# A hybrid encoder kernel: the exponent rows of the SSD kept twice in memory and loaded by head, and two columns of the input projection moved ahead of four others

## The chip, the cores and the metric

The kernel runs on one core of a Trainium2 chip. The metric is the device time of one execution in microseconds (us). Five engines work beside each other, each in its own order: TensorE (PE) multiplies matrices, VectorE (DVE) and ScalarE (ACT) work element by element, GpSimd (POOL) here mostly issues the DMA loads and stores of activations, SyncE (SP) the loads of weights. They meet at semaphores.

## The reference, cut to what matters

Two sequences of 512 and 256 positions pass through two layers. A layer is one input projection, three branches (a bidirectional state space branch, called SSD here, a windowed attention and a long convolution, called hyena), and one output projection.

```
h = rms_norm(x, norm_g);  u = h @ w_in
z, xbc, dt_raw, q, k, v, g_att, hy_proj, g_hy = split(u)
y_ssd = ssd_branch(z, xbc, dt_raw, ...)      # forward scan + the same on the flipped sequence
y_att = attention_branch(q, k, v, g_att, ...)
y_hy  = hyena_branch(hy_proj, g_hy, ...)     # irfft(rfft(u) * rfft(kern)), times a gate
x = x + concat([y_ssd, y_att, y_hy]) @ w_out

# ssd_scan, on chunks of 128 positions (512 = 4 chunks, 256 = 2 chunks), 16 heads of 64 channels
a_cs   = cumsum(dt * a)                                   # the exponent rows, per head and chunk
y_diag = (cm . bm * exp(a_cs[l] - a_cs[s]), l >= s) @ (x * dt)
y_off  = cm @ prev_state * exp(a_cs)                      # prev_state: scan over chunks
y      = y_diag + y_off
```

## The kernel before, in words

All 768 positions are held at once, 2048 channels as 16 operand tiles. Values are split in a high and a low part (`hi`, `lo` for weights, OPH and OPL for the operand), so that a product is three matmuls. `gemm_col` computes one column of 128 outputs: 16 operand tiles x 2 position halves (PSUM tiles `gs` and `gq`) x 3 products = 96 matmuls of 384 columns. It goes in four quarters of 24 matmuls. ACT makes a `hi` from a raw weight tile (`ACTIVATE hi<-raw`), DVE the `lo` (`lo<-raw,hi`), for 12 matmuls at a time; three buffers of each let the two engines run ahead of PE.

Everything else is background work: generators (`ssd_gen`, `filter_gen`, `hyena_gen`, `att_gen`) from which `gemm` takes one step after each quarter (`bg.step`), and small jobs in the middle of a quarter (`bg.half`, which runs what `bg.mid` holds). Instructions are written in that order. A list scheduler then sets the order on each engine by the order of writing, with weights and their splits raised. Every engine runs its list strictly in order, so an instruction that waits holds all behind it. `bg.flush(g)` runs a generator to its end at once.

The parts that the change touches, with the names that the rows use:

- `ssd_gen` (from L604). The cumulated exponents of 2 directions x 16 heads x 6 chunks are stored to memory as `rows_d` (six stores, L638). Then eight `pair`s of heads run, a new one every fifth step, each in eight steps. A pair loads its rows three times by two (L684, `t<-rows_d`, 256 KB, each row repeated over 128 partitions). It loads them once more for the factor exp(a_cs) of `y_off` (L726), called E2 here: two tiles of 128 partitions x 512, the first 64 partitions for the first head and the others for the second. Each tile takes two loads, of three chunks and of one, and their source is a hand-made address pattern whose outermost size is 2 (heads) and whose second is a 64-fold repeat. `load(out=t, in_=xs_d)` (L746) fetches the branch's input. Three steps later ACT takes the exponential (`t<-t 128x512`, L138) of each tile. In the step after it come the pair's two groups of matmuls into `yS` and `yP` (`m`), and in the last step DVE adds up (`XS<-s,prm_t,m`, the only reader of these two PSUM banks, and `XS<-XS,t`).
- After the columns of the SSD and of the hyena's inputs come the SSD's gates, columns 20 to 27. `scale_ssd` then multiplies the eight tiles XS by a row and stores each (`ys_d<-XS`, L1037).
- Columns 28 to 31 are the hyena's gates. Before a column is used, `bg.flush(hy[j // 2])` runs what is left of a half of the hyena. That half ends with the inverse transform: 48 matmuls `m<-r,t`, whose `r` are split by ACT (`r<-t`) and DVE from four loads of `in_ivS` (L588).
- `new_xs(F32R)` gives the XS buffer anew; its writers wait until all readers of the old one are done, the eight stores to `ys_d` among them. Column 32 (keys) writes `KH` into it by four ACT copies (`XS<-s 64x768`), column 33 (values) fills `vt`. Then attention and the columns 34 to 37 follow.
- All `load`s of activations stand in one queue on POOL, in order.

Of the kernel before, what the change touches and what calls it, by code (L numbers as in the profile page):

```python
# [11 lines left out]
F32 = mybir.dt.float32  # L12
F32R = mybir.dt.float32r
# [6 lines left out]
DEPTH = 2  # L20
TH = 384
D = 2048
SL, PL = 512, 256
# [74 lines left out]
def trunk(ctx: ExitStack, tc: tile.TileContext, xT, w_in, w_dt, w_out, prm, brow, w1, mlpv, w2, w3, w4,  # L98
# [22 lines left out]
    def t2(shape=(128, 512), dt=F32):  # L121
        return t2p.tile(list(shape), dt, tag="t2", name="t2")
# [4 lines left out]
    def TT(o, a, b, op, eng=None):  # L127
        (eng or nc.vector).tensor_tensor(out=o, in0=a, in1=b, op=op)  # L128
# [5 lines left out]
    def STT(o, a, s, b, op0, op1, eng=None):  # L134
        (eng or nc.vector).scalar_tensor_tensor(out=o, in0=a, scalar=s, in1=b, op0=op0, op1=op1)  # L135
# [33 lines left out]
    def new_xs(dt=F32):  # L169
        xs_tile[:] = [big.tile([128, 8 * T], dt, tag="XS", name="XS")]  # L170

    def XS(j, a=0, b=T):
        return xs_tile[0][:, T * j + a:T * j + b]
# [6 lines left out]
    fb_d = drp.tile([8, 128, 512], F32, name="fb_d")  # L180
    f0_d = drp.tile([8, 512], F32, name="f0_d")
    rows_d = drp.tile([DEPTH, 2, 16, NCH, 128], F32, name="rows_d")
    ys_d = drp.tile([DEPTH, 8, 128, T], F32, name="ys_d")
    xs_d = drp.tile([DEPTH, 8, 128, T + GAP], F32, name="xs_d")

# [2 lines left out]
    def P(l, base, i):  # L188
        c = l * NPRM + base + i
        return prm_t[:, c:c + 1]  # L190
# [85 lines left out]
    def gemm_col(src, consume):  # L276
        out = banks()
        gemm([src], [out])
        consume(*out)
# [324 lines left out]
    def ssd_gen(l, dtT, BT, CT, ready):  # L604
# [22 lines left out]
        TT(adt, dt, bc(na, (128, 2, NCH, 16)), MUL)  # L627
        yield
        yield
        for b in range(3):  # L630
            p = mp((16, 4, 128))
            for i in range(4):
                c, d = divmod(4 * b + i, 2)
                MM(p[:, i, :], adt[:, d, c, :], tri_t[:, d, :])
            r = t2((16, 4, 128))
            nc.scalar.copy(out=r, in_=p)
            for d in range(2):
                load(out=rows_d[l, d, :, 2 * b:2 * b + 2, :],  # L638
                     in_=r.rearrange("h (c d) t -> h d c t", d=2)[:, d])
        p = mp((128, 2, 2, NCH, 16))  # L640
        for d in range(2):
            MM(p[:, 0, d], tri_t[:, d, :], adt[:, d])
# [10 lines left out]
        TS(acs[:, 1], acs[:, 1], -1.0, MUL)  # L653
        yield
        yield

        FW, BW = (0, 1, 2, 4), (1, 2, 3, 5)

        def group(g):
            bt, cbF, cbB = s3((128, NCH, 128)), s3((128, NCH, 128)), s3((128, NCH, 128))  # L660
# [13 lines left out]
        def pair(j, bt, cbF, cbB):  # L674
# [44 lines left out]
            prep(0, R0)  # L719
            R2 = rows(2)  # L720
            E2 = []
            for d, cs in ((0, BW), (1, FW)):
                t = t2((128, 4, 128))
                for i, n in ((0, 3), (3, 1)):
                    src = rows_d[l, d, h0:h0 + 2, cs[i]:cs[i] + n, :]
                    load(out=t[:, i:i + n, :], in_=bass.AP(src.tensor, src.offset,  # L726
                         [[NCH * 128, 2], [0, 64], [128, n], [1, 128]]))
                E2.append(t)
            yield
            H = [t2((128, 4, 2, 64)), t2((128, 4, 2, 64))]  # L730
# [23 lines left out]
            for c in range(NCH):  # L754
                for hh in range(2):
                    hs = slice(64 * hh, 64 * hh + 64)
                    o = yS[hs, c, :] if c < 4 else yP[hs, c - 4, :]
                    MM(o, X[:, c, hh, :], Ms[c // 2][:, hh, c % 2, :])
            yield
            dsk = P(l, PDS, j)  # L760
            yT = Xf.rearrange("p (c t) -> p c t", c=NCH)
            STT(yT[:, 0:4], t[:, 0:SL].rearrange("p (c t) -> p c t", c=4), dsk, yS, MUL, ADD)
            STT(yT[:, 4:6], t[:, SL + GAP:T + GAP].rearrange("p (c t) -> p c t", c=2), dsk, yP, MUL, ADD)
            for d, cs in ((0, BW), (1, FW)):
                for i, n in ((0, 3), (3, 1)):
                    c = cs[i]
                    TT(yT[:, c:c + n], yT[:, c:c + n], E2[d][:, i:i + n], ADD)
            yield

        act, nxt, gt = [], 0, None  # L770
# [196 lines left out]
    for l in range(DEPTH):  # L967
# [57 lines left out]
        for j in range(8):  # L1025
            def f(ps, pq):
                z = silu2(ps, pq, rstd)
                y = XS(j)
                TT(y, y, z, MUL)
                square_acc(y, acc, j == 0)  # L1030
# [5 lines left out]
                TT(y, y, r, MUL)  # L1036
                load(out=ys_d[l, j], in_=y)  # L1037
        rms(acc, 1024, eps4, 2, scale_ssd)
        for j in range(4):
            def f(ps, pq):  # L1040
                bg.flush(hy[j // 2])
                a = hconv(j, ps, pq)
                TT(yh[j][:, 0:SL], yh[j][:, 0:SL], a[:, 0:SL], MUL)
                TT(yh[j][:, SL:T], yh[j][:, SL:T], a[:, SL + GAP:T + GAP], MUL)
            gemm_col(W(28 + j), f)

        new_xs(F32R)
        KH = [XS(6), XS(7)]
        kL = s3p.tile([128, T], F32R, tag="s3", name="kL")
        KL = [(kL[:, 0:SL], kL[:, SL:T]), (t2((128, SL), F32R), t2((128, PL), F32R))]  # L1050

        def f(ps, pq):
            k = s3()
            evac(lambda a, b: k[:, a:b], ps, pq, rstd)
            for g in range(2):
                ks = k[64 * g:64 * g + 64]
                for o in (g, 1 - g):
                    ACT(KH[g][64 * o:64 * o + 64], ks, AF.Copy)
                hi = KH[g][64 * g:64 * g + 64].bitcast(F32)
                for o in (g, 1 - g):  # L1060
                    for t, a, b in zip(KL[g], (0, SL), (SL, T)):
                        TT(t[64 * o:64 * o + 64], ks[:, a:b], hi[:, a:b], SUB)
# [3 lines left out]
        def f(ps, pq):  # L1066
# [8 lines left out]
                    nc.scalar.copy(out=vt[:, 3 * b:3 * b + 3, :], in_=p)  # L1075
            bg.later(4, turn)
        gemm_col(W(33), f)
        qs, QA = [], [[XS(2 * i % 6), XS(2 * i % 6 + 1)] for i in range(4)]
        bg.add(att_gen(l, qs, QA, KH, KL, vt))
        for i in range(4):  # L1080
# [193 lines left out]
```

## Time and profile before

| | us |
|---|---|
| median of 3 runs | 2487.45 (2485.87 to 2487.83) |
| the profiled execution | 2489.0 |
| its span in the trace | 2487.2 |
| PE busy in the span | 2441.4 |
| DVE busy | 1580.5 |
| ACT busy | 1087.5 |
| POOL busy | 341.4 |

PE is busy nearly all the time, so the time is PE's work, at the clock that was granted, plus PE's gaps. The busy time of another engine counts only where PE waits for it. The list of waits of PE therefore is the list of what could be saved, and the granted clock (PEclk, 1.00 is 2.4 GHz, 0.50 is 1.2 GHz) is the second thing to look at.

### The profile page before, as it was taken

The page shows a single profiled execution, that of the slowest core. Times are in us where ns is not written, and L with a number is a line of the kernel's source. Part 1 is how long each engine was busy: PE and PEld are TensorE (multiplying, and loading weights), DVE is VectorE, ACT ScalarE, POOL GpSimd, SP SyncE. Part 2 cuts the span into 40 slices and gives each one's busy share as a digit, 9 for nine tenths or more (in the row PEclk, how much of TensorE's full clock was granted, in tenths as well). Part 3 has the DMA queues.
Part 4 walks back from the last instruction along what each step waited for, and adds up shares of the span by engine and source line. Part 5 has one row for each costly group of instructions (what it writes and reads, how often), then busy time and mean ns, then how long its engine had stood idle before and what let it go on. Part 6 is the DMA issues. An engine that isn't in the chain of part 4 may idle for free.

```text
span 2487.2 us, 40924 instructions
## 1 busy us (share of the span) xinstructions
PE 2441.4 (98%) x15066; PEld 2393.2 (96%) x15066; DVE 1580.5 (64%) x3410; ACT 1087.5 (44%) x2560; POOL 341.4 (14%) x683
## 2 busy tenths in 40 slices
PE   8999999999999999999999999999999999999998
PEld 7999999999999999999999999999999999999997
DVE  6888775558856766544476787766746477573333
ACT  6467653334334444333353575633332355352332
POOL 2033221221100010121200332201001000000001
PEclk9999999999999999999999999999999999999999
DMA  4266542443421132344421555423213111332223
GB/s 169 63 153 146 142 129 86 129 133 124 140 78 60 51 100 80 112 149 132 146 96 55 141 149 149 135 85 106 94 60 128 63 54 47 106 109 89 77 82 132
DMA packets 126921, 266.22 MB, mean 107 GB/s; under 512 B 30175, under 2 KB 36666, under 8 KB 126720
## 3 DMA queue, kind: packets, MB, share of 16 engines
q1 hardware_dynamic: 78048, 136.35, 17.7%
q0 software_dynamic: 48672, 127.26, 17.2%
q8 instruction: 118, 1.93, 0.3%
q14 instruction: 83, 0.68, 0.1%
HBM read 231.23 MB, written 34.18 MB: 107 GB/s over the span
## 4 chain that ended last, share of the span: by engine, by line
PE 90%; DMA 4%; issue 2%; DVE 1%; ACT 1%; POOL 1%; DVEq 0%; ACTq 0%; POOLq 0%
PE gs L141 38%; PE gq L141 38%; PE m L141 12%; DMA t<-rows_d 3%; PE m L848 1%; PE gl L141 1%; POOL t L726 0%; ACT t L138 0%; DMA XS<-in_xT 0%; DMA s<-in_xT 0%; ACT hi L138 0%; DVE lo L128 0%; DVE t L135 0%; PE m L1000 0%; DVE t L128 0%
## 5 line engine op out<-in xcount | busy, mean ns | idle before, releaser
L138 ACT ACTIVATE hi<-raw 128x256 fp32r<-128x256 f32 x984 | 405.6, 414 | 1040.1 <-PE gq L141 920.5
L128 DVE TENSOR_TENSOR lo<-raw,hi 128x256 fp32r<-128x256 f32 x984 | 412.5, 421 | 597.9 <-ACT hi L138 587.0
L141 PE MATMUL gs<-OPH,hi 128*128 128x384 f32 x1920 | 657.4, 342 | 18.1 <-ACT OPH L138 11.0
L141 PE MATMUL gs<-OPH,lo 128*128 128x384 f32 x1920 | 645.0, 336 | 0.6 <-DVE lo L128 0.5
L141 PE MATMUL gq<-OPH,lo 128*128 128x384 f32 x1920 | 644.4, 336 | 0.0
L141 PE MATMUL gs<-OPL,hi 128*128 128x384 f32 x1920 | 644.0, 336 | 0.1
L141 PE MATMUL gq<-OPH,hi 128*128 128x384 f32 x1920 | 644.1, 335 | 0.0
L141 PE MATMUL gq<-OPL,hi 128*128 128x384 f32 x1920 | 643.3, 335 | 0.0
L141 PEld LDWEIGHTS gs<-OPH,hi 128*128 128x128 f32 x1920 | 362.4, 189 | 25.2 <-ACT OPH L138 11.3
L141 PEld LDWEIGHTS gs<-OPH,lo 128*128 128x128 f32 x1920 | 361.6, 188 | 2.7 <-DVE lo L128 2.7
L141 PEld LDWEIGHTS gs<-OPL,hi 128*128 128x128 f32 x1920 | 362.3, 189 | 0.8 <-DVE OPL L135 0.6
L141 PEld LDWEIGHTS gq<-OPH,hi 128*128 128x128 f32 x1920 | 361.8, 188 | 0.0
L141 PEld LDWEIGHTS gq<-OPL,hi 128*128 128x128 f32 x1920 | 361.6, 188 | 0.0
L141 PEld LDWEIGHTS gq<-OPH,lo 128*128 128x128 f32 x1920 | 361.5, 188 | 0.0
L128 DVE TENSOR_TENSOR t<-t,t 128x512 f32<-128x512 f32 (+3 forms) x260 | 169.1, 668 | 26.5 <-ACT t L138 23.6
L135 DVE SCALAR_TENSOR_TENSOR s<-cv,prm_t,s 128x770 f32<-128x770 f32 x144 | 145.9, 1015 | 22.6 <-ACT s L138 21.9
L138 ACT ACTIVATE t<-s,dt 128x128 f32<-128x128 f32 x384 | 133.6, 391 | 18.9 <-DVE t L135 18.5
L128 DVE TENSOR_TENSOR s<-s,s 128x768 f32<-128x768 f32 (+2 forms) x126 | 112.8, 904 | 27.3 <-ACT s L138 26.7
L138 ACT ACTIVATE t<-t 128x512 fp32r<-128x512 f32 (+3 forms) x132 | 77.3, 587 | 92.4 <-DMA t<-rows_d 48.6
L128 DVE TENSOR_TENSOR t<-m,t 128x256 f32<-128x256 f32 (+3 forms) x157 | 72.3, 485 | 18.3 <-PE m L141 5.8
L684 POOL DMA_DIRECT2D t<-rows_d x96 | 68.8, 719 | 103.9 <-DVE XS L128 38.0
L138 ACT ACTIVATE t<-t,acs 128x128 f32<-128x128 f32 x192 | 73.6, 389 | 13.6 <-DVE t L135 13.6
(225 smaller groups left out, 2572.6 us busy)
## 6 DMA issues: line engine op xcount, KB each, us to landing
raw<-in_w_in SPq DMA_DIRECT2D x368, 256.0 KB, 3.0
raw<-in_w_out SPq DMA_DIRECT2D x128, 256.0 KB, 3.0
t<-rows_d POOLq DMA_DIRECT2D x96, 256.0 KB, 6.4
s<-in_xT POOLq DMA_DIRECT2D x24, 384.0 KB, 4.4
xs_d<-s POOLq DMA_DIRECT2D x16, 385.0 KB, 4.2
s<-xs_d POOLq DMA_DIRECT2D x16, 385.0 KB, 9.3
t<-rows_d POOLq DMA_DIRECT2D x32, 192.0 KB, 10.5
t<-in_decay POOLq DMA_DIRECT2D x24, 256.0 KB, 4.9
```

Of the source, the lines that this page charges most:

```text
L128: (eng or nc.vector).tensor_tensor(out=o, in0=a, in1=b, op=op)
L135: (eng or nc.vector).scalar_tensor_tensor(out=o, in0=a, scalar=s, in1=b, op0=op0, op1=op1)
L138: nc.scalar.activation(o, i, f, **kw)
L141: nc.tensor.matmul(o, lhsT=l, rhs=r, start=start, stop=stop)
L684: load(out=t, in_=rows_d[l, d, h0:h0 + 2, 2 * u:2 * u + 2, :].partition_broadcast(128))
L848: nc.tensor.transpose(pt[g][:, 128 * kb:128 * kb + 128], s[g][:, 128 * kb:128 * kb + 128], ident)
```

## The change

Three things are changed.

First, a second tensor `ed_d` holds the exponent rows in the order in which E2 reads them: per direction and head four chunks of 128. Six more stores a layer fill it, beside those to `rows_d`. E2's loads become one for each tile and head, 128 KB of the row of one head, repeated over 64 partitions. There are four loads a pair, as before.

Second, the last step of a pair becomes a function `final` that is put into `bg.mid`. The pair's generator ends one step sooner.

Third, the columns 32 and 33 are computed ahead of 28 to 31, and the new XS buffer is taken inside the use of column 32.

```diff
--- before.py
+++ after.py
@@ -180,6 +180,7 @@
     fb_d = drp.tile([8, 128, 512], F32, name="fb_d")
     f0_d = drp.tile([8, 512], F32, name="f0_d")
     rows_d = drp.tile([DEPTH, 2, 16, NCH, 128], F32, name="rows_d")
+    ed_d = drp.tile([DEPTH, 2, 16, 4, 128], F32, name="ed_d")
     ys_d = drp.tile([DEPTH, 8, 128, T], F32, name="ys_d")
     xs_d = drp.tile([DEPTH, 8, 128, T + GAP], F32, name="xs_d")
 
@@ -627,6 +628,7 @@
         TT(adt, dt, bc(na, (128, 2, NCH, 16)), MUL)
         yield
         yield
+        FW, BW = (0, 1, 2, 4), (1, 2, 3, 5)
         for b in range(3):
             p = mp((16, 4, 128))
             for i in range(4):
@@ -635,8 +637,11 @@
             r = t2((16, 4, 128))
             nc.scalar.copy(out=r, in_=p)
             for d in range(2):
-                load(out=rows_d[l, d, :, 2 * b:2 * b + 2, :],
-                     in_=r.rearrange("h (c d) t -> h d c t", d=2)[:, d])
+                v = r.rearrange("h (c d) t -> h d c t", d=2)[:, d]
+                load(out=rows_d[l, d, :, 2 * b:2 * b + 2, :], in_=v)
+                cs = [(i, c - 2 * b) for i, c in enumerate((BW, FW)[d]) if c // 2 == b]
+                i, c = cs[0]
+                load(out=ed_d[l, d, :, i:i + len(cs), :], in_=v[:, c:c + len(cs)])
         p = mp((128, 2, 2, NCH, 16))
         for d in range(2):
             MM(p[:, 0, d], tri_t[:, d, :], adt[:, d])
@@ -654,8 +659,6 @@
         yield
         yield
 
-        FW, BW = (0, 1, 2, 4), (1, 2, 3, 5)
-
         def group(g):
             bt, cbF, cbB = s3((128, NCH, 128)), s3((128, NCH, 128)), s3((128, NCH, 128))
             for b in range(2):
@@ -719,12 +722,10 @@
             prep(0, R0)
             R2 = rows(2)
             E2 = []
-            for d, cs in ((0, BW), (1, FW)):
+            for d in range(2):
                 t = t2((128, 4, 128))
-                for i, n in ((0, 3), (3, 1)):
-                    src = rows_d[l, d, h0:h0 + 2, cs[i]:cs[i] + n, :]
-                    load(out=t[:, i:i + n, :], in_=bass.AP(src.tensor, src.offset,
-                         [[NCH * 128, 2], [0, 64], [128, n], [1, 128]]))
+                for hh in range(2):
+                    load(out=t[64 * hh:64 * hh + 64], in_=ed_d[l, d, h0 + hh].partition_broadcast(64))
                 E2.append(t)
             yield
             H = [t2((128, 4, 2, 64)), t2((128, 4, 2, 64))]
@@ -756,15 +757,16 @@
                     hs = slice(64 * hh, 64 * hh + 64)
                     o = yS[hs, c, :] if c < 4 else yP[hs, c - 4, :]
                     MM(o, X[:, c, hh, :], Ms[c // 2][:, hh, c % 2, :])
-            yield
-            dsk = P(l, PDS, j)
-            yT = Xf.rearrange("p (c t) -> p c t", c=NCH)
-            STT(yT[:, 0:4], t[:, 0:SL].rearrange("p (c t) -> p c t", c=4), dsk, yS, MUL, ADD)
-            STT(yT[:, 4:6], t[:, SL + GAP:T + GAP].rearrange("p (c t) -> p c t", c=2), dsk, yP, MUL, ADD)
-            for d, cs in ((0, BW), (1, FW)):
-                for i, n in ((0, 3), (3, 1)):
-                    c = cs[i]
-                    TT(yT[:, c:c + n], yT[:, c:c + n], E2[d][:, i:i + n], ADD)
+            def final():
+                dsk = P(l, PDS, j)
+                yT = Xf.rearrange("p (c t) -> p c t", c=NCH)
+                STT(yT[:, 0:4], t[:, 0:SL].rearrange("p (c t) -> p c t", c=4), dsk, yS, MUL, ADD)
+                STT(yT[:, 4:6], t[:, SL + GAP:T + GAP].rearrange("p (c t) -> p c t", c=2), dsk, yP, MUL, ADD)
+                for d, cs in ((0, BW), (1, FW)):
+                    for i, n in ((0, 3), (3, 1)):
+                        c = cs[i]
+                        TT(yT[:, c:c + n], yT[:, c:c + n], E2[d][:, i:i + n], ADD)
+            bg.mid.append(final)
             yield
 
         act, nxt, gt = [], 0, None
@@ -1036,20 +1038,13 @@
                 TT(y, y, r, MUL)
                 load(out=ys_d[l, j], in_=y)
         rms(acc, 1024, eps4, 2, scale_ssd)
-        for j in range(4):
-            def f(ps, pq):
-                bg.flush(hy[j // 2])
-                a = hconv(j, ps, pq)
-                TT(yh[j][:, 0:SL], yh[j][:, 0:SL], a[:, 0:SL], MUL)
-                TT(yh[j][:, SL:T], yh[j][:, SL:T], a[:, SL + GAP:T + GAP], MUL)
-            gemm_col(W(28 + j), f)
-
-        new_xs(F32R)
-        KH = [XS(6), XS(7)]
-        kL = s3p.tile([128, T], F32R, tag="s3", name="kL")
-        KL = [(kL[:, 0:SL], kL[:, SL:T]), (t2((128, SL), F32R), t2((128, PL), F32R))]
+        KH, KL = [], []
 
         def f(ps, pq):
+            new_xs(F32R)
+            KH.extend((XS(6), XS(7)))
+            kL = s3p.tile([128, T], F32R, tag="s3", name="kL")
+            KL.extend(((kL[:, 0:SL], kL[:, SL:T]), (t2((128, SL), F32R), t2((128, PL), F32R))))
             k = s3()
             evac(lambda a, b: k[:, a:b], ps, pq, rstd)
             for g in range(2):
@@ -1075,6 +1070,14 @@
                     nc.scalar.copy(out=vt[:, 3 * b:3 * b + 3, :], in_=p)
             bg.later(4, turn)
         gemm_col(W(33), f)
+        for j in range(4):
+            def f(ps, pq):
+                bg.flush(hy[j // 2])
+                a = hconv(j, ps, pq)
+                TT(yh[j][:, 0:SL], yh[j][:, 0:SL], a[:, 0:SL], MUL)
+                TT(yh[j][:, SL:T], yh[j][:, SL:T], a[:, SL + GAP:T + GAP], MUL)
+            gemm_col(W(28 + j), f)
+
         qs, QA = [], [[XS(2 * i % 6), XS(2 * i % 6 + 1)] for i in range(4)]
         bg.add(att_gen(l, qs, QA, KH, KL, vt))
         for i in range(4):
```

How instructions move, at three places.

The first place is POOL's queue in layer 0, where the second pair's loads are issued. `h_d<-s` is the store of an intermediate of the filter's network; `s<-xs_d`, `t<-rows_d` and `t<-ed_d` are the pair's loads. Before:

```order
L375 DMA h_d<-s_1643 128x768
L746 DMA s_1714<-xs_d 128x770
L684 DMA t_1832<-rows_d 128x2x256
L684 DMA t_1834<-rows_d 128x2x256
L684 DMA t_1915<-rows_d 128x2x256
L684 DMA t_1917<-rows_d 128x2x256
L726 DMA t_1919<-rows_d 128x1x384
L726 DMA t_1919<-rows_d 128x1x128
L726 DMA t_1922<-rows_d 128x1x384
L726 DMA t_1922<-rows_d 128x1x128
```

After:

```order
L687 DMA t_1839<-rows_d 128x2x256
L747 DMA s_1721<-xs_d 128x770
L687 DMA t_1841<-rows_d 128x2x256
L687 DMA t_1922<-rows_d 128x2x256
L687 DMA t_1924<-rows_d 128x2x256
L728 DMA t_1926<-ed_d 64x512 x2
L728 DMA t_1929<-ed_d 64x512 x2
L118 MEMSET cv 128x2 x3
L376 DMA h_d<-s_1650 128x768
```

The store `h_d<-s` stood ahead of all these loads and now stands behind them.

The second place is ACT's list in layer 0, at the end of the hyena's second half, where the inverse's splits `r<-t` stand; `t_7424<-t_7412` and the like are the other operand of the same matmuls. Before:

```order
L526 COPY t_7399<-m 128x256
L527 COPY t_7399<-m 128x256
L138 ACTIVATE hi<-raw 128x256 x3
L138 ACTIVATE t_7424<-t_7412 128x512
L138 ACTIVATE t_7428<-t_7413 128x512
L138 ACTIVATE r_7436<-t_7434 128x512
L138 ACTIVATE r_7442<-t_7440 128x512
L138 ACTIVATE r_7472<-t_7470 128x512
L138 ACTIVATE r_7478<-t_7476 128x512
```

After:

```order
L527 COPY t_7413<-m 128x256
L528 COPY t_7413<-m 128x256
L138 ACTIVATE hi<-raw 128x256 x5
L138 ACTIVATE t_7487<-t_7475 128x512
L138 ACTIVATE t_7491<-t_7476 128x512
L138 ACTIVATE hi<-raw 128x256 x2
L138 ACTIVATE r_7499<-t_7497 128x512
L138 ACTIVATE r_7505<-t_7503 128x512
L138 ACTIVATE r_7603<-t_7601 128x512
L138 ACTIVATE r_7609<-t_7607 128x512
```

Between the last copies of the forward transform and the inverse's splits stood three weight splits, and now stand seven. On PE the 48 matmuls of this inverse came 35 weight matmuls behind the last of the forward transform, and now come 81 behind; the first half's inverse stood 80 behind in the kernel before.

The third place is ACT's list in layer 1, behind the last row of the SSD's norm (`s<-m,eps`). Before, the first gate of the hyena followed:

```order
L138 ACTIVATE s_19771<-m,eps_93 128x512
L138 ACTIVATE s_19771<-m,eps_93 128x256
L138 ACTIVATE hi<-raw 128x256 x8
L138 ACTIVATE s_19940<-cv,prm_t 128x770
L138 ACTIVATE hi<-raw 128x256 x4
```

After, the four key copies into the new XS buffer:

```order
L138 ACTIVATE s_19784<-m,eps_93 128x512
L138 ACTIVATE s_19784<-m,eps_93 128x256
L138 ACTIVATE hi<-raw 128x256 x9
L138 ACTIVATE XS<-s_19950 64x768
L138 ACTIVATE hi<-raw 128x256
L138 ACTIVATE XS<-s_19950 64x768 x2
L138 ACTIVATE hi<-raw 128x256
L138 ACTIVATE XS<-s_19950 64x768
L138 ACTIVATE hi<-raw 128x256 x9
```

The copies stand one column behind the norm, between weight splits; in the kernel before they came four columns later. On PE the order of the weight matmuls and of the SSD's matmuls around them is as before. On DVE the pair's last step (`XS<-s,prm_t,m`) stands behind the same weight matmul in both kernels.

## Rows read from the trace of the kernel before

**Rows 1.** Page, busy time: us (share of the span) and instructions.

```profile
PE 2441.4 (98%) x15066; PEld 2393.2 (96%) x15066; DVE 1580.5 (64%) x3410; ACT 1087.5 (44%) x2560; POOL 341.4 (14%) x683
```

**Rows 2.** Waits of PE, whole span: us in total, times, longest us.

```profile
PE m L141 <- DVE XS L135: 7.9, 2, 4.0
PE gs L141 <- ACT hi L138: 6.5, 5, 2.1
PE m L141 <- ACT r L138: 4.6, 1, 4.6
```

**Rows 3.** Timeline of PE: start, us, instruction [idle before, releaser].

```profile
276.36 0.80 PE L141 MATMUL m<-t,s 128*128 128x128 f32 x2 [4.00 <-DVE XS L135]
...
355.21 0.45 PE L141 MATMUL gs<-OPH,hi 128*128 128x384 f32 x1 [1.44 <-ACT hi L138]
...
1604.95 0.45 PE L141 MATMUL gs<-OPH,hi 128*128 128x384 f32 x1 [2.03 <-ACT hi L138]
```

**Rows 4.** Waits of ACT, the row on the exponent rows: us, times, longest.

```profile
ACT t L138 <- DMA t<-rows_d: 48.6, 24, 4.7
```

**Rows 5.** Timeline of ACT, at E2's exponentials.

```profile
274.25 0.63 ACT L138 ACTIVATE t<-t 128x512 f32<-128x512 f32 x1 [2.00 <-DMA t<-rows_d]
274.79 1.01 ACT L138 ACTIVATE hi<-raw 128x256 fp32r<-128x256 f32 x3
...
1603.96 0.63 ACT L138 ACTIVATE t<-t 128x512 f32<-128x512 f32 x1 [3.08 <-DMA t<-rows_d]
```

**Rows 6.** Timeline of DVE behind them.

```profile
275.22 0.42 DVE L128 TENSOR_TENSOR lo<-raw,hi 128x256 fp32r<-128x256 f32 x1 [7.89 <-ACT hi L138]
```

**Rows 7.** Timeline of POOL: issues of E2's loads, and the store ahead of them.

```profile
165.35 0.56 POOL L375 DMA_DIRECT2D h_d<-s  x1 [11.02 <-ACT hi L138]
...
262.43 3.23 POOL L726 DMA_DIRECT2D t<-rows_d  x4 [0.35 <-issue]
...
1592.90 3.22 POOL L726 DMA_DIRECT2D t<-rows_d  x4 [3.36 <-PE m L141]
```

**Rows 8.** Page, DMA issues: count, KB each, median us from issue to landing.

```profile
t<-rows_d POOLq DMA_DIRECT2D x96, 256.0 KB, 6.4
t<-rows_d POOLq DMA_DIRECT2D x32, 192.0 KB, 10.5
...
ys_d<-XS POOLq DMA_DIRECT2D x16, 384.0 KB, 4.8
...
rows_d<-t POOLq DMA_DIRECT2D x12, 16.0 KB, 2.7
```

**Rows 9.** Windows: length, busy of PE, PEld, DVE, ACT, POOL; PEclk, DMA share, GB/s.

```profile
1600.20:1602.20 2.00, 2.00 (x22) 1.75 (x22) 0.00 (x0) 0.64 (x1) 0.00 (x0) 1.00 0.19 61
1587.00:1590.00 3.00, 3.00 (x20) 3.00 (x19) 3.00 (x10) 1.29 (x4) 1.42 (x2) 1.00 0.71 203
```

**Rows 10.** Windows behind five of PE's gaps, columns as above.

```profile
189.90:193.40 3.50, 3.47 (x11) 3.21 (x12) 3.47 (x9) 3.50 (x11) 0.00 (x0) 0.52 0.22 75
276.30:282.10 5.80, 5.74 (x23) 5.74 (x24) 4.64 (x14) 2.55 (x7) 0.72 (x1) 0.51 0.33 88
...
695.60:702.00 6.40, 6.38 (x28) 6.08 (x29) 5.32 (x12) 3.11 (x5) 1.23 (x5) 0.51 0.09 12
1526.60:1531.60 5.00, 4.99 (x25) 4.99 (x26) 3.84 (x11) 1.75 (x5) 0.72 (x1) 0.66 0.33 95
1604.90:1612.00 7.10, 7.05 (x34) 6.89 (x35) 5.09 (x15) 5.55 (x19) 0.00 (x0) 0.76 0.36 120
```

**Rows 11.** Timeline of PE, inverse transforms of the hyena's second and first half.

```profile
695.61 8.94 PE L141 MATMUL m<-r,t 128*128 128x256 f32 x48 [4.58 <-ACT r L138]
...
619.57 2.65 PE L141 MATMUL m<-r,t 128*128 128x256 f32 x21
```

**Rows 12.** Timeline of POOL in layer 1, the last store of the SSD's output.

```profile
1878.79 0.54 POOL L1037 DMA_DIRECT2D ys_d<-XS  x1 [0.67 <-DVE XS L128]
```

**Rows 13.** Timeline of ACT in layer 1, a weight split just behind.

```profile
1885.12 0.42 ACT L138 ACTIVATE hi<-raw 128x256 fp32r<-128x256 f32 x1 [1.67 <-PE gq L141]
```

## The prediction

> **What bounds the kernel now.** I read the page's busy times first. PE is busy 2441.4 us of a span of 2487.2 [rows 1], so 45.8 us are PE's gaps, and the rest of the engines matter only where they make one. Next the waits of PE. Three of their rows stand in the part of the program that is changed [rows 2]: 7.9 us in two waits for DVE's last step of a pair, 6.5 us in five waits for a weight split `hi`, 4.6 us in one wait for the hyena's `r`. The other 26.8 us of gaps are not on the change's path, and I leave them alone.
>
> The timelines say what these gaps are. The reader should follow one from the end. At 276.36 PE had waited 4.00 us for a PSUM bank that DVE's last step frees [rows 3]. DVE had stood idle for 7.89 us, not with that step but with the weight split `lo` ahead of it, which waited for ACT's `hi` [rows 6]. ACT made that `hi` at 274.79, right behind the exponential of the second E2 tile, and this had waited for its load [rows 5]. The load had been issued from 262.43 on [rows 7]. So PE's gap is the landing of E2, 11.8 us after the first of four issues, and DVE and ACT only hand it on. The other gaps have the same chain: 1604.95 with an exponential at 1603.96 and loads issued from 1592.90 (11.1 us), 355.21 [rows 3], and the second wait for DVE's step, before 1526.6 [rows 2, 10]. In all ACT waits 48.6 us in 24 waits for such rows [rows 4]; most of these waits are absorbed by splits made ahead, the rest is PE's.
>
> Behind the gaps comes a second cost. The granted clock is 0.51 in the 5.8 us after the gap of 276.36, and 0.52, 0.51, 0.66 and 0.76 in the stretches after four others [rows 10]: PE ran at 1.2 GHz in a part of each of these stretches, where 2.4 GHz is full speed.
>
> **The change, part by part.**
>
> *E2 by head.* Needed first: how early must the tiles land? At 276.36 a last exponential 4.00 us earlier starts at 270.25, 7.8 us after the first issue. At 1604.95 it is 2.03 us earlier, 1601.9, or 9.0 us after it [rows 3, 5, 7]. How long will the new loads take? No row has a 64-partition load of repeated rows. The nearest above is the 256 KB load of `rows_d` over 128 partitions, 6.4 us against 10.5 for the old 192 KB load [rows 8]: the smaller old load is the slower one. The nearest below is the 16 KB store, 2.7 us [rows 8]. A new load moves 128 KB. Halfway between the two is 4.6 us, and the last of four is issued three times 0.81 us behind the first (3.23 us for four [rows 7]), so it lands after some 7.0 us; with the whole 6.4 us it is 8.8. The first is in time at both places, the second is 1 us late at the earlier one and in time at the other. What speaks for the lower value: the old load runs narrow. While only its tail was under way the DMA share was 0.19 at 61 GB/s, where `rows_d` loads of the ordinary form run at 0.71 and 203 GB/s [rows 9].
>
> The Trainium skill has a rule for that: its page "DMA: Bandwidth & Descriptors", section "Rules for kernel authors", says that an outermost size below 16 confines a transfer to at most that many engines. The old pattern has 2 outermost, the new one 64; the share of 0.19 agrees with a narrow transfer.
>
> So the gain is both waits for DVE's step, 7.9, and of the 6.5 us of `hi` waits 5.5: 2.03 and 1.44 [rows 3], and the longest, 2.1 [rows 2], before 189.9. That last one also has another remedy: the store `h_d` held POOL 11.02 us until 165.35 [rows 7] with all of the second pair's loads behind it, and now stands behind them. I leave 1 us out of the 6.5, two small waits that I don't follow. Sum 13.4; for the residue above I take off 0.6 (bounds 0 and 2).
>
> *The clock* comes back with the gaps. One minus the clock, times the length, is 1.7, 2.8, 3.1, 1.7 and 1.7 over the five windows [rows 10], 11.0 in all. The window says a bit too much: 48 matmuls of the inverse took 8.94 us, where 21 at full speed took 2.65, or 6.06 for 48 [rows 11]. That is 2.9 lost where the window says 3.1. With this factor 10.2, of which 3.1 x 0.92 = 2.9 belong to the hyena's gap and 7.3 to E2's.
>
> *Stores.* Six stores a layer of under 16 KB, each about 0.54 us of issue on POOL as another store takes [rows 12], 3 us a layer. They stand between the six to `rows_d`, ahead of the first pair's loads. What hides them is PE's own columns, which ask nothing of POOL. Cost 0; if the first pair's loads come 3 us later and nothing takes it up, 3 us a layer, which I count in the upper end.
>
> *The last step in `bg.mid`.* DVE's order of this step is the same, so it neither moves the step nor frees the banks sooner. What it does: the generator ends 24 matmuls sooner, and the filter's work in layer 0 starts sooner and mixes differently. Value 0.5 lost, bounds 2 either way, the size of the small gaps that work has now.
>
> *Keys and values first.* The gain is at the hyena's second half in layer 0. Its inverse stood 35 weight matmuls behind the forward, with four splits `r` in a row behind the last loads, and PE waited 4.6 us [rows 2, 11]. Now the distance is 81, as at the first half, whose inverse at 619.57 runs on without a gap [rows 11]. So 4.6 go, and with them 2.9 of clock. Layer 1 has no such gap and gains nothing.
>
> The price is a new wait. The four key copies on ACT write the new XS buffer and so wait for all eight stores to `ys_d`. The last is issued at 1878.79 [rows 12] and lands 4.8 us later by the median [rows 8], at 1883.6. The first copy stands 18 weight matmuls behind that issue. A matmul of 256 columns takes 0.126 us (21 in 2.65 [rows 11]), one of 384 then some 0.19, so 18 are 3.4 us, and ACT waits about 1.4. Queued behind it is `hi`, and behind that PE. ACT waited 1.67 us for PE to free a buffer before a `hi` in this stretch [rows 13], so it is as far ahead as the buffers let it. Two full ones hold 24 matmuls, 4.6 us of work. A wait of 1.4 is covered. If the last store landed 4 us later than the median, 1 us would be missing; I put the bound at 4 us a layer, and take 0.5 for both.
>
> **Sum.** 13.4 - 0.6 (E2) + 4.6 (hyena) + 10.2 (clock) - 0.5 (filter) - 0.5 (keys) = 26.6. The profiled execution took 2489.0, so 2462.4; it lies 1.55 above the median of the runs. Forecast 2460.9, say 2461. Own range 2457 to 2465.
>
> **Rivals.**
>
> B, the loads only get halfway: they land 1 to 2 us late at the tight places, gaps of 1 to 2 us stay at three of them and with them some clock. 5 to 11 us are lost of the 26.6, 2466 to 2472. For it: each pair's tiles stand behind other loads in one queue, and their issue isn't earlier. Against: the 9.0 us at one of the two places.
>
> C, the keys' wait: it exceeds the cover, 2 to 4 us a layer plus a low clock of 1.7 to 3 behind each [rows 10], 5 to 14 in all, 2466 to 2475. For it: the eight stores are issued 1 us apart and queue among themselves. Against: ACT's idle time before each split [rows 13].
>
> D, the new loads are no faster, since a load into 64 partitions gains nothing on one into 128. Then E2's gaps and their clock stay, and only the hyena's 4.6 + 2.9 and little else is won: 2480 to 2481.
>
> The Trainium skill speaks for D: "SBUF — State Buffer", section "Door 1", has 64 partitions reach only half of the ports, and the rules of the DMA page advise against splitting a transfer into partition halves. By that the 6.4 us of a full load would hold for each half or be doubled. No row here shows a 64-partition load large enough to say.
>
> E, slower: the same mechanism, but the new loads land later than the old. It decides from about 13 us after the first issue, against 11.8 now: of the 24 waits of ACT [rows 4] twelve end a pair, and if each grows by 1.1 us and PE pays it, the 7.5 us of the hyena and 5 us more are lost. At 15 us the time would be 2489 - 8 + 12 x 3.2, about 2518. For it only the halves; against it the narrow old pattern [rows 9].
>
> F, the change doesn't do what it says: for the second part this is my forecast (the order is the same); for the first it is D.
>
> **How the numbers follow.** Forecast 0.68, B 0.12, C 0.10, D 0.06, E 0.04. The likeliest is the forecast, 2461. The range reaches down to 2456 (the filter's 2 us and a residue of 0) and up over most of B and C, to 2474. A measurement of this kernel can tell about 0.2%, 5 us, from no change. Faster is below 2482.5: the forecast, B, C and most of D, 0.91. Within 0.2%: the slower side of D, the milder of E, 0.05. Slower 0.04.
>
> **What would show it.** Right: the waits of PE of the changed kernel have no row of 3 us or more for DVE's last step and none for `r`; ACT's wait for `ed_d` is below 15 us in all, against 48.6; the new loads' median to landing is below 6.4 us; PEclk is 1.00 between 150 and 2400 us. Wrong: ACT's wait for `ed_d` near 40 (D); a row of ACT waiting for the `ys_d` stores with PE waiting for `hi` behind it (C); new gaps in the filter's stretch around 500 to 560 us.

## The result and the profile after

The changed kernel took 2458.23 us (median of four, 2457.56 to 2459.86) against 2487.34 for the kernel before on the same chip: ratio 0.9885 (0.9868 to 0.9902), 29.1 us less. The forecast was 2461, its own range 2457 to 2465. The time is right, in part by luck: in the profiled execution the keys cost 5.0 us more than forecast, and misses of 2.7, 1.7 and some 3.6 us the other way made up for it.

The waits of PE over the whole span, after (us in total, times, longest):

```profile
PE gs L141 <- ACT OPH L138: 10.8, 2, 9.7
PE m L141 <- ACT t L138: 2.0, 3, 1.0
PE m L141 <- DVE t L128: 1.9, 1, 1.9
PE m L141 <- DVE s L128: 1.1, 1, 1.1
PE gs L141 <- DVE lo L128: 0.6, 1, 0.6
...
```

The three rows of [rows 2] are gone. The largest left is the start, which the change doesn't touch. The 1.9 us for `t` are new.

ACT's wait for the exponent rows, which was 48.6 us [rows 4], and the page's rows on the loads (count, KB each, median us to landing), after:

```profile
ACT t L138 <- DMA t<-ed_d: 3.3, 5, 1.5
```

```profile
t<-rows_d POOLq DMA_DIRECT2D x96, 256.0 KB, 6.1
...
t<-ed_d POOLq DMA_DIRECT2D x64, 128.0 KB, 6.4
```

The place that the prediction followed, on POOL and on ACT, after:

```profile
256.69 2.08 POOL L728 DMA_DIRECT2D t<-ed_d  x4
```

```profile
261.98 0.62 ACT L138 ACTIVATE t<-t 128x512 f32<-128x512 f32 x1
262.91 0.63 ACT L138 ACTIVATE t<-t 128x512 f32<-128x512 f32 x1 [0.31 <-DMA t<-ed_d]
```

The second exponential starts 6.2 us after the first issue, where it started 11.8 us after [rows 5, 7]. By the prediction it may start up to 7.8 us after it without a gap on PE, and there is none here. The four loads took 3.8 to 4.6 us each from issue to landing. Half of the pairs' loads, issued right behind loads of `rows_d`, took 7.5 to 10.8 us, so the median is 6.4. Four windows over the SSD's stretches (length, busy of PE, PEld, DVE, ACT, POOL; PEclk, DMA share, GB/s) show PE busy nearly throughout and the clock at 1.00, i.e. 2.4 GHz:

```profile
150.00:240.00 90.00, 89.29 (x599) 86.79 (x599) 81.78 (x196) 65.29 (x185) 27.26 (x60) 1.00 0.60 163
240.00:380.00 140.00, 139.76 (x940) 136.97 (x939) 110.45 (x266) 82.32 (x233) 33.84 (x74) 1.00 0.48 137
1360.00:1560.00 200.00, 200.00 (x1344) 197.09 (x1343) 170.91 (x411) 136.89 (x390) 55.51 (x116) 1.00 0.58 156
1560.00:1640.00 80.00, 80.00 (x524) 79.16 (x523) 54.98 (x122) 34.60 (x91) 9.82 (x28) 1.00 0.33 104
```

**Where the time went.** Each of the 11648 weight matmuls `gs` and `gq` stands in all traces. The start of the same-numbered one says what a stretch gave against the profiled execution of the kernel before, its clock included. The last column is a second execution of the changed kernel, the run `e8_after` of the next section.

| stretch | weight matmuls | us, after minus before | second execution |
|---|---|---|---|
| start | 0 to 624 | -1.8 | -1.3 |
| SSD pairs, layer 0 | 624 to 1488 | -12.5 | -11.1 |
| filter and hyena's first half, layer 0 | 1488 to 2832 | -2.2 | -2.4 |
| key copies, layer 0 | 2832 to 2904 | +5.5 | +2.0 |
| hyena's second half, layer 0 | 2904 to 3144 | -7.0 | -7.1 |
| rest of layer 0, start of layer 1 | 3144 to 6528 | -1.3 | -1.4 |
| SSD pairs, layer 1 | 6528 to 7416 | -9.3 | -9.6 |
| rest | 7416 to the end | -0.5 | -0.5 |

The start is not the change's: a gap of 1.2 us that stands there in every execution ended between 16.4 and 18.5 us, in kernels that are alike there.

The +5.5 is the price of the keys in this execution. ACT, DVE and PE there, after, in three views:

```profile
633.73 2.57 ACT L138 ACTIVATE XS<-s 64x768 fp32r<-64x768 f32 x3 [3.64 <-DMA t<-in_fwS]
636.33 0.42 ACT L138 ACTIVATE hi<-raw 128x256 fp32r<-128x256 f32 x1
...
638.27 0.61 ACT L138 ACTIVATE t<-t 128x512 fp32r<-128x512 f32 x1
```

```profile
634.61 2.05 DVE L128 TENSOR_TENSOR kL<-s,XS 64x512 fp32r<-64x512 f32 x4 [3.08 <-ACT XS L138]
...
641.16 0.69 DVE L128 TENSOR_TENSOR t<-t,t 128x512 fp32r<-128x512 f32 x1
```

```profile
638.94 0.73 PE L141 MATMUL m<-r,t 128*128 128x256 f32 x4 [0.80 <-ACT t L138]
641.90 0.79 PE L141 MATMUL m<-r,t 128*128 128x256 f32 x2 [1.88 <-DVE t L128]
```

ACT waited 3.64 us before the first key copy. The view names a load of `in_fwS`, but the two such loads under way landed at 634.15 and 634.78, after the copy had begun; the last store to `ys_d` was issued at 627.28 and landed at 633.43, 0.3 us before it. Behind the copies stood the split `t<-t`, which the forward transform of the hyena's second half waits for (two expectations below call it an inverse; the first half's inverse was done by 607 us). DVE's second half of that split came behind the eight subtractions for the keys. PE was without work twice, 2.7 us in all, and the window behind the second gap has the clock at 0.57:

```profile
641.90:648.70 6.80, 6.80 (x28) 6.80 (x29) 2.44 (x6) 1.47 (x4) 0.00 (x0) 0.57 0.13 42
```

In layer 1 ACT waits at the same place, but only weight splits stand behind the copies there, and PE has no gap:

```profile
1855.01 0.85 ACT L138 ACTIVATE XS<-s 64x768 fp32r<-64x768 f32 x1 [2.79 <-DMA t<-fb_d]
```

### The profile page after: what moved, and what is told of

Read it like the earlier page. It is cut to its first block, busy times and chain, and to the rows that moved or that the text cites. A ratio compares the mean times of both kernels' runs of the same rounds, so it can differ in the third digit from the quotient of the medians.

```text
span 2458.1 us, 40960 instructions
## 1 busy us (share of the span) xinstructions
PE 2430.2 (99%) x15066; PEld 2384.6 (97%) x15066; DVE 1583.1 (64%) x3410; ACT 1088.3 (44%) x2560; POOL 327.9 (13%) x695
## 4 chain that ended last, share of the span: by engine, by line
PE 92%; issue 3%; DMA 2%; DVE 1%; POOL 1%; ACT 1%; DVEq 0%; POOLq 0%; ACTq 0%
PE gs L141 39%; PE gq L141 38%; PE m L141 13%; PE m L850 1%; PE gl L141 1%; DMA t<-rows_d 1%; DMA t<-in_fwS 0%; PE m L1002 0%; DMA t<-in_w 0%; DMA prm_t<-in_prm 0%; ACT t L138 0%; DVE dt L135 0%; DMA XS<-ys_d 0%; PE m L502 0%; DVE s L135 0%
## 5 line engine op out<-in xcount | busy, mean ns | idle before, releaser
L141 PE MATMUL gs<-OPH,hi 128*128 128x384 f32 x1920 | 655.7, 342 | 11.0 <-ACT OPH L138 10.8
L141 PEld LDWEIGHTS gs<-OPH,hi 128*128 128x128 f32 x1920 | 361.5, 188 | 16.9 <-ACT OPH L138 11.1
```

What stands on the lines that cost most here:

```text
L141: nc.tensor.matmul(o, lhsT=l, rhs=r, start=start, stop=stop)
```

## The experiments

The theory: the old E2 loads were slow because of their address pattern; the keys pay a wait for the stores; the rest follows. The rivals: the order in memory or the place in the queue made the old loads slow; the keys' own work makes the gap; the last step in the middle of a quarter has a part in the gain.

**Each part alone.** The first: `ed_d`, its stores and the loads by head, all else as before.

> The kernel before with the second tensor ed_d and the loads by head alone (last step and columns as before). If the E2 loads were the cause of the gaps before matmuls of the SSD, all of them go with their low clock and nothing else changes: between the same weight matmuls of layer 0 and layer 1 some 22 us less than before, 2463 to 2467 us; the gap of 4.6 us before the hyena's inverse stays. If the gain of the whole change came in part from the last step in the middle of a quarter, less: 2470 or more.

Measured 2464.74 us against 2489.46, ratio 0.9904 (0.989 to 0.9919), 24.7 less. ACT waited 3.3 us for `ed_d`. The rows of PE's waits for DVE's last step and for `hi` were gone, and the row for the hyena's `r` stood as before. In the profiled execution the two stretches of the pairs took 14.0 and 9.0 us less. So this part carries most of the gain, and by itself.

```profile
ACT t L138 <- DMA t<-ed_d: 3.3, 4, 1.8
```

```profile
PE m L141 <- ACT r L138: 4.6, 1, 4.6
```

The third: the columns 32 and 33 ahead of 28 to 31.

> The kernel before with the key and value columns ahead of the hyena's gates alone. Theory: the gap of 4.6 us before the inverse of the second half goes with 3 us of clock (7.5 us), and a new one comes at the key copies, which wait for the stores to ys_d, 5.4 us with its clock: net 2 us, 2484 to 2486. If the key copies cost nothing by themselves and the gap in the changed kernel had another cause: 2479 to 2481.

Measured 2486.01, ratio 0.9989 (0.998 to 0.9999), 3.4 less. The wait for `r` was gone, and the gap of 1.9 us for `t` at the keys was there, without a low clock behind it. In the profiled execution the hyena's stretch took 5.5 us less and the keys' 1.1 more, so here the keys paid back a part of the gain, not most of it. Another 2.0 went in the stretch behind.

```profile
PE m L141 <- DVE t L128: 1.9, 1, 1.9
```

The second: the last step in `bg.mid`.

> The kernel before with the pair's last step in the middle of a quarter alone. DVE's order of that step is the same, so the gaps at the pairs stay as they are (7.9 us for DVE's last step, 6 to 7 us for hi). What can move is the filter's work of layer 0, which starts one quarter sooner: if the 1.8 us of small waits between 480 and 580 us that the changed kernel does not have went with it, 2 us less than before; if they went with another part, no difference and the waits are still there.

Measured 2483.17, ratio 0.9973 (0.9964 to 0.9982), 6.2 less, where I had forecast next to nothing and then expected 2. Of the waits between 480 and 580 us only one row of 1.4 us was left. The more interesting row is the hyena's second inverse, which this part doesn't name at all. PE, timeline:

```profile
689.94 0.51 PE L141 MATMUL m<-r,t 128*128 128x256 f32 x2 [2.83 <-ACT r L138]
```

The gap was 4.58 [rows 11], and 3.4 us at 1.2 GHz followed it, where 6.8 had. The order of the instructions says why: the generator of a pair ends a quarter sooner, all background work behind it moves up, and the second half's forward transform ends 48 weight matmuls ahead of its inverse, not 35. By the weight matmuls this part took 2.0 us out of the filter's stretch and 3.0 out of 2832 to 3144; the start's scatter of 1.8 was lost again in other stretches, so its profiled execution gained 4.9 in all. The pairs' own gaps stayed, 4.4 us for DVE's last step and 1.7 for `hi` between 240 and 380 us; there the step itself moved nothing.

The other side of it, the changed kernel without that part:

> The changed kernel without the last step in the middle of a quarter: the loads by head and the key and value columns ahead. If that step is worth 2 us in the filter's stretch: 2460 to 2461 us, and the three small waits for s, r and t between 480 and 580 us are there. If nothing: the time of the changed kernel.

Measured 2461.24, ratio 0.9885 (0.9872 to 0.9898), on a chip where the kernel before took 2489.36. Against the changed kernel that is 0 by the ratio and 3 us by the medians of two chips, so the times don't settle it. The traces do. In the ten profiled executions of kernels with the step in `bg.mid` the filter's stretch (1488 to 2832) took 0.6 to 2.8 us less than before, in the three without it between 0.2 less and 0.7 more. And the waits of 480 to 580 us are back as in the kernel before (PE's waits of that stretch):

```profile
PE m L141 <- ACT t L138: 2.4, 2, 1.7
PE gs L141 <- DVE s L128: 0.6, 1, 0.6
PE m L502 <- DVE r L128: 0.6, 1, 0.6
```

The hyena's second inverse comes 81 weight matmuls behind the forward transform in this run too. So in the changed kernel the step is worth its part in the filter's stretch, 2 to 3 us; what it gave at the hyena alone, the columns give without it.

**What made the old loads slow.** E2 still from `ed_d`, in one load a tile, with the old kind of pattern:

```diff
-                for hh in range(2):
-                    load(out=t[64 * hh:64 * hh + 64], in_=ed_d[l, d, h0 + hh].partition_broadcast(64))
+                src = ed_d[l, d, h0:h0 + 2]
+                load(out=t, in_=bass.AP(src.tensor, src.offset, [[512, 2], [0, 64], [1, 512]]))
```

> The changed kernel, E2 still read from ed_d, but each tile in one load of 256 KB whose source has 2 heads outermost and the 64-fold repeat second, as the old loads had. If the outermost size of 2 makes the load narrow: median to landing 10 us or more, ACT waits 30 us or more for ed_d, the gaps return, 2472 to 2482 us. If the old loads were slow because of their order in memory, their pieces of one chunk or their place in the queue: to landing near 6.4 us, as in the changed kernel, 2457 to 2460.

Measured 2490.99 against 2489.46, ratio 1.0008 (0.9998 to 1.0017): the whole gain is gone, which is more than I had expected. The pairs' stretches took 5.6 and 8.9 us more than before, and only the hyena's 7.0 less stayed. ACT's wait, the page's row on the load, and a window in which the two loads of the last pair were the only ones under way:

```profile
ACT t L138 <- DMA t<-ed_d: 52.1, 16, 7.2
```

```profile
t<-ed_d POOLq DMA_DIRECT2D x32, 256.0 KB, 11.6
```

```profile
1602.50:1605.00 2.50, 2.50 (x17) 2.50 (x15) 0.00 (x0) 0.00 (x0) 0.00 (x0) 1.00 0.25 93
```

The median to landing was 11.6 us. The DMA share of 0.25 is that of 4 of 16 engines for two loads, two for each. The Trainium skill says this in "DMA: Bandwidth & Descriptors", section "Rules for kernel authors": an outermost size below 16 holds a transfer to at most as many engines. This run agrees, with a size of 2 and two engines a load. I had taken the four loads of the kernel before for the measure of the pattern and forgot that two loads have half the engines of four.

One gap didn't come back with the old kind of pattern, the one before 189.9 with its low clock [rows 2, 10]:

```profile
180.00:195.00 15.00, 15.00 (x96) 15.00 (x95) 14.79 (x33) 10.77 (x31) 4.74 (x7) 1.00 0.52 123
```

These loads stand ahead of the store `h_d`, as in the changed kernel. So that gap, 2.1 us and 1.7 of clock, goes with the place in the queue and not with the pattern; no run moves the store alone.

The next run asks for the number of loads, with four of equal size:

```diff
-                load(out=t, in_=bass.AP(src.tensor, src.offset, [[512, 2], [0, 64], [1, 512]]))
+                for i in (0, 2):
+                    src = ed_d[l, d, h0:h0 + 2, i:i + 2, :]
+                    load(out=t[:, i:i + 2, :], in_=bass.AP(src.tensor, src.offset,
+                         [[512, 2], [0, 64], [128, 2], [1, 128]]))
```

> The changed kernel, E2 from ed_d, each tile in two loads of 128 KB for both heads, two chunks each, with 2 heads outermost and the 64-fold repeat second: four loads a pair as in the kernel before, but of equal size. If each such load is held to two of the 16 DMA engines, four in flight use up to eight, against four with one load a tile (DMA share 0.25 there): DMA share up to 0.5 with nothing else under way, ACT waits less than the 52 us there but much more than the 3 us of the changed kernel, 2468 to 2484 us. If the two engines are shared by all four loads: as slow as with one load a tile, 2488 us or more.

Measured 2473.09 against 2489.99, ratio 0.9933 (0.9915 to 0.995). ACT's wait for the tiles, the page's row on the loads, a window in which the four loads of the last pair were the only ones under way, and PE's wait for DVE's last step:

```profile
ACT t L138 <- DMA t<-ed_d: 33.5, 16, 5.4
```

```profile
t<-ed_d POOLq DMA_DIRECT2D x64, 128.0 KB, 9.4
```

```profile
1584.00:1585.00 1.00, 1.00 (x7) 1.00 (x7) 0.81 (x2) 0.00 (x0) 0.00 (x0) 1.00 0.50 131
```

```profile
PE m L141 <- DVE XS L135: 6.4, 2, 3.8
```

The share is 0.50 with four loads, twice that of two. So the same bytes in the same pattern are faster in four loads than in two, and with the repeat outermost faster again: 2491, 2473, 2458. No run has the old loads of three chunks and of one beside the other two parts, so what equal sizes give by themselves is not shown. The remaining rival is the order in memory. The changed kernel with its loads by head, but from `rows_d`, in the old pieces of three chunks and one:

```diff
+            for d, cs in ((0, BW), (1, FW)):
                 for hh in range(2):
-                    load(out=t[64 * hh:64 * hh + 64], in_=ed_d[l, d, h0 + hh].partition_broadcast(64))
+                    for i, n in ((0, 3), (3, 1)):
+                        load(out=t[64 * hh:64 * hh + 64, i:i + n, :],
+                             in_=rows_d[l, d, h0 + hh, cs[i]:cs[i] + n, :].partition_broadcast(64))
```

> The changed kernel without ed_d in E2's path: the loads go by head into 64 partitions, but from rows_d in the old order, in pieces of three chunks and of one, so eight loads a pair instead of four. If the address pattern (the repeat outermost) is what makes the new loads fast: each lands in 6 us or less, eight issues take 4.3 us instead of 2.1, the tiles come about 2 us later than in the changed kernel, ACT waits 5 to 15 us for them, 2458 to 2464 us. If the order in memory (one run of four chunks a head) is what does it: to landing near 10 us, the gaps return, 2475 us or more.

Measured 2461.68 against 2488.74, ratio 0.989 (0.9873 to 0.9906); ACT waited 5.6 us, and the loads landed 4.2 us after their issue by the median. The changed kernel on the same chip took 2458.33. So the loads by head give nearly the whole gain without the second tensor. That tensor, with four loads a pair in place of eight, is worth some 3 us by the medians, and the intervals overlap; in the profile that shows as one gap in the second pair, PE's timeline:

```profile
192.91 1.13 PE L141 MATMUL m<-s,t 128*128 128x128 f32 x8 [1.68 <-DVE t L135]
```

**What the keys pay for.** Column 28 ahead of the keys and values, so that the stores have a column more to land:

```diff
+        for j in range(1):
+            ...
+            gemm_col(W(28 + j), f)
         KH, KL = [], []
...
         gemm_col(W(33), f)
-        for j in range(4):
+        for j in range(1, 4):
```

> The changed kernel with column 28 ahead of the keys and values: 28, 32, 33, 29, 30, 31. If the gap of some 2.9 us at 638 to 642 us with its low clock comes from the key copies that wait for the last store to ys_d, one column of 16.6 us more lets the stores land: no wait of ACT before the key copies, 5 us less than the changed kernel, 2452 to 2454. If it comes from the first half's own inverse and its splits: the same 2458, or the gap moves.

Measured 2453.06 (2452.51 to 2459.96) against 2489.46, ratio 0.9864 (0.9849 to 0.9878). To compare it with the changed kernel on one chip, both ran again:

> The changed kernel once more, on the same chip as the next one, to compare the two: ratio to the kernel before 0.988 to 0.989, with the gap and the low clock at the keys in layer 0.

> Column 28 ahead of the keys and values once more. If the wait for the stores cost the changed kernel 5.4 us: 4 to 6 us less than the changed kernel on this chip, no wait of ACT before the key copies in layer 0. If the gain seen before was the chip's: within 2 us of it.

Measured 2458.33 (2456.80 to 2459.28) for the changed kernel and 2455.28 (2455.12 to 2456.89) for the other, ratios 0.9877 (0.9861 to 0.9893) and 0.9868 (0.9849 to 0.9887). With the column ahead ACT had no wait before the key copies, and in the changed kernel it had:

```profile
645.00 1.71 ACT L138 ACTIVATE XS<-s 64x768 fp32r<-64x768 f32 x2
```

```profile
634.61 2.58 ACT L138 ACTIVATE XS<-s 64x768 fp32r<-64x768 f32 x3 [2.84 <-DMA t<-in_fwS]
```

The gain is 3 us here, not 4 to 6. The profile of the changed kernel says why: its longer gap at the keys was there, the one of 0.80 us ahead of it was not, and no low clock followed. PE's timeline there, and a window over it:

```profile
642.78 0.50 PE L141 MATMUL m<-r,t 128*128 128x256 f32 x2 [1.87 <-DVE t L128]
```

```profile
640.00:647.00 7.00, 5.13 (x34) 4.81 (x35) 5.12 (x12) 1.48 (x4) 0.00 (x0) 1.00 0.22 71
```

With two columns ahead (28 and 29):

> The changed kernel with both gates of the hyena's first half ahead of the keys and values: 28, 29, 32, 33, 30, 31. If only the landing of the stores to ys_d matters, as good as one column ahead: 3 to 5 us less than the changed kernel. If the four columns between the forward and the inverse of the second half are needed, the gap of 4.6 us before that inverse comes back in part: slower than with one column ahead.

Measured 2454.69 against 2489.36, ratio 0.9858 (0.9845 to 0.9871). No gap for `r`, and PE without one at the old place of the keys:

```profile
635.00:650.00 15.00, 15.00 (x93) 14.72 (x92) 13.39 (x30) 4.52 (x11) 1.07 (x2) 1.00 0.29 87
```

One column ahead and two are the same by their intervals. Both have medians 3 to 5 us below the changed kernel's. The intervals of the ratios overlap with its interval; on the one chip that both saw, three of four runs with one column ahead lay below all runs of the changed kernel. They are the fastest versions here.

The column moves the key work as well as the wait. So one more: the keys in two tiles of their own, in the changed kernel's order.

```diff
-            KH.extend((XS(6), XS(7)))
+            KH.extend(s3p.tile([128, T], F32R, tag="s3", name="kh") for _ in range(2))
```

> The changed kernel with the keys in two tiles of their own in place of the new XS buffer, columns in the order of the changed kernel, so that the key copies no longer have the stores to ys_d ahead of them. If that wait makes the gap before the hyena's first inverse: ACT no longer waits 3.6 us before the copies, PE's 2.8 us of gaps between 637 and 642 us and the low clock behind them go, some 5 us less than the changed kernel. If the work of the keys itself (four ACT copies, eight DVE subtractions) makes it: no change.

Measured 2463.76 against 2488.74, ratio 0.99 (0.9882 to 0.9918): 5 us more than the changed kernel on this chip, not 5 less. Yet the mechanism shows. ACT began the key copies without a wait, right behind a split:

```profile
632.21 0.42 ACT L138 ACTIVATE hi<-raw 128x256 fp32r<-128x256 f32 x1 [1.94 <-DVE s L128]
632.68 3.44 ACT L138 ACTIVATE kh<-s 64x768 fp32r<-64x768 f32 x4
```

The two gaps at the keys were gone; between weight matmuls 2832 and 3144 it took 5.4 us less than the first profiled execution of the changed kernel, and 2.0 less than the second, which ran on this chip. More than that was lost 240 us later, and once in layer 1, where there was no gap before, each time with 3.4 us at 1.2 GHz. PE's row on them, whole span:

```profile
PE gs L141 <- DVE s L128: 5.3, 2, 2.7
```

The two tiles come from the pool of 14 that `s` comes from, and they stay until attention is done. That the wait was for a tile of this pool fits, but no run shows it.

## Why the prediction was right, point by point

- **E2 by head**, 13.4 less 0.6, and 7.3 of clock: 20.1 forecast. The two stretches of the SSD's pairs gave 12.5 + 9.3 = 21.8 in one execution and 20.6 in the other, and the part alone 24.7 by the medians. The step held: landing 6.2 us after the first issue at the place that was worked out, 7.0 forecast, with 4.6 us for the last load, as estimated, and issues 0.52 us apart where 0.81 was taken. So did the reason, a narrow load. In [rows 9] it is narrower than I read it: weight loads were under way in that window too, and by the packets make 1.3 of its 3.1 busy engines. Rival D, no gain from loads into 64 partitions, didn't show: at 1567.66 four loads with nothing else of theirs in the queue landed within 5.0 us of the first issue, the second exponential following at 1573.03 without a wait. One sign that I named was missed: the median to landing is 6.4, not below it, since half of the loads stand right behind others.
- **The clock**, 10.2 forecast. Where gaps went, it was 1.00 in all four windows. The sign of 1.00 up to 2400 us was missed at the keys: 6.8 us at 1.2 GHz in one execution, none in the other.
- **The last step in `bg.mid`**, 0.5 lost with bounds of 2: wrong in sign and size. Alone it gave 6.2 us, and in the changed kernel 2 to 3. I had checked the order of the moved step, found it unchanged, and stopped there. What I costed loosely, that all later background work starts a quarter sooner, was the effect: the filter's small waits, and, in the run by itself, the hyena's distance from 35 to 48.
- **Keys and values first**, gain 7.5: 7.0 measured. Price 0.5: 5.5 in one profiled execution, 2.0 in the other. The 5.5 is what rival C, with a chance of 0.10, gave a single layer; layer 1 had no gap. C's argument, stores that queue among themselves, held: in layer 0 the first landed 2.8 us after its issue, the last 6.2, where I took the median of 4.8. ACT waited 3.64 and 2.79 us in the two layers where I had worked out 1.4. The cover that I named, splits of weights made ahead, held even so, and C's sign, PE waiting for `hi`, didn't come. The step that failed is the list of what stands behind the copies. I read it in layer 1, where it is weight splits alone, and took layer 0 to be alike. There the hyena's split `t<-t` stands in it, and PE waited for that.
- **Sum.** In the first profiled execution the misses were +5.0 at the keys, +0.5 at the hyena, -2.7 in the filter's stretch, -1.7 at E2, and -3.6 in stretches that I left at zero and that include the start's scatter. That they nearly cancel is luck. Two sums at the edges were wrong as well: E's last one gives 2519, not 2518, and the two terms named for the lower end reach 2457.8, not 2456.

## What to carry to other kernels

Where a load repeats rows over partitions, write its address pattern so that the repeat is outermost; with two rows outermost the same bytes landed after 9.4 us in four loads and 11.6 in two, against 6.4 by head. From the old order in memory it was 10.5 us, and 4.2 by head, in smaller pieces. Before a step is costed at nothing because it keeps its place, look at what stands behind it in its generator. And where a buffer is taken over from one that is being stored, list every instruction that is queued behind its first writer, in each layer apart.

## What the runs showed of the hardware

Two loads with an outermost size of 2 made a DMA share of 0.25, four such loads 0.50.

At the keys the same kernel ran with a low clock in one execution and without in another. In the first PE had gaps of 0.80 and 1.88 us, 3 us apart; the clock fell inside the second, and PE ran 6.8 us at 1.2 GHz. In the other it had one of 1.87 us alone, and the clock stayed at 2.4 GHz. The stretch cost 5.5 us in the first and 2.0 in the second, so whether the small gap is there differs between executions of one kernel, and the low clock with it. The run with four narrow loads had gaps of 0.85 and 1.87 us at this place, and the clock fell there too:

```profile
650.20:653.60 3.40, 3.40 (x12) 3.40 (x11) 1.72 (x5) 1.47 (x4) 0.00 (x0) 0.50 0.10 28
```

The key columns alone had 0.45 and 1.87 us there, and it stayed at 2.4 GHz. I had priced the clock by each gap alone. Three more executions had 0.33 us or nothing ahead of a gap of 1.73 to 1.86, at 2.4 GHz too. That the gap ahead decides fits them all; no run was made to test it.
